# Input loaded in 2 KB rows and transposed before the norm, modulation matmuls of a whole column block in one burst, in a two-layer diffusion kernel

## The chip, the cores and the metric

The kernel runs on one core of a Trainium2 chip. The core has five engines that run their own lists of instructions in order and wait for each other by semaphores: TensorE (PE, matrix products into PSUM, with weight loads shown apart as PEld), VectorE (DVE), ScalarE (ACT), GpSimd (POOL) and SyncE (SP), which here only issues DMAs. Sixteen DMA engines move the data between HBM and the on-chip memory. The metric is the device time of one launch in microseconds. Three runs of the kernel before gave 2896.36, 2903.05 and 2905.09 us; the median is 2903.05.

## What is computed

Two layers of a diffusion backbone over 512 latent tokens `x` and 256 context tokens `ctx`, width 2048, all in float32. Each layer norms its input, modulates it by shift and scale that come from a vector `c` (latent) or `c_ctx` (context) through `w_ada`, projects it through `w_in` to queries, keys, values and a gate path z, runs three groups of attention heads, gates, projects back through `w_out` and adds the result to its input under a third modulation.

```python
shift, scale, gate = jnp.split(sc @ w_ada[l] + b_ada[l], 3, axis=-1)
...
h = rms(x, norm_w[l]) * (1.0 + scale[:, None]) + shift[:, None]
hc = rms(xc, norm_w[l]) * (1.0 + scale_c) + shift_c
...
qa, ka, va, qb, kb, vb, qc, kc, vc, z = project_stream(h, *weights, rope=(cos, sin))
```

`w_ada` is 2048 x 6144 for each layer, 50 MB in float32; shift and scale are its first two thirds, 33.5 MB. x is 4.2 MB and ctx 2.1 MB.

## The kernel before

Matrix products need the contracted dimension on the 128 partitions. So the normed, modulated input is kept transposed, as 16 k tiles `hT[.][k]`: 128 columns of the width on the partitions, the 768 tokens beside each other. Each float32 factor is split into a rounded half and the rest (`hi`, `lo`, or `wh`, `wl` for weights), and each product takes three matmuls: hi by hi, hi by lo, lo by hi (`mm`, line 333).

The start of layer 0 has these parts. `load_x` (line 854) loads x and ctx by k tile: 128 tokens by 128 columns, so rows of 512 bytes, two DMAs for each k tile; ACT squares it and DVE sums the squares by token. `ada_scale` (line 829) walks over shift and scale in blocks of 256 columns, alternating; `ada_blocks` (line 708) loads each block in eight tiles of 256 KB into the pool `s3` and multiplies them with the vectors in `scT` (line 743). Four tiles make one group of matmuls; up to 12 are loaded ahead. `ada_finish` brings the result onto the partitions (line 760), and `ada_use` adds the bias and makes the scale. `make_h` (line 870) waits for all squares, forms the norm's factor for each token, and `make_hk` multiplies a k tile by it, transposes it on PE (`tr`, line 336), and modulates it into `hT`.

The jobs of the projection then run in a list. In layer 0 the first is a pair: the first half (k tiles 0 to 7) of a key/value chunk and of a query chunk of 256 columns, in steps of two k tiles (`TJob.step`); the 72 matmuls of one such pair of steps have 256 columns each. Behind them stand three z jobs (`FJob`, 216 matmuls of 384 columns up to the end of modulation), then the second halves.

The order is made when the program is built. Strands (Python generators) put out instructions one by one, and a planner (`Weaver`) picks the next from a model of the engines' times; each engine then runs its list as it stands. All loads from HBM that matter here go through SP's one queue, in the order in which they were put out. A DMA into a buffer that is still read waits in SP's queue, and everything behind it waits too. The weights of the jobs come through `loader` and `splitter`: three buffers `ws` for loads, and two buffers `wl` for the rests, which come free when PE has used them. `RES` keeps some `s3` buffers back from the modulation's loads.

At the change of layers `post_out` (line 1872) makes the next input tile, its squares, and stores it to `xs1`.

## Time and profile before

| what | us |
|---|---|
| median of three runs | 2903.05 |
| the profiled execution | 2901.62 |
| its span | 2899.8 |
| PE busy in the span | 2775.4 |
| DVE busy in the span | 1995.0 |
| PE busy from 0 to 200 us | 154.0 |
| PE busy from 200 to 400 us | 197.3 |

The profile is of one execution. A line of a group names the line of the program, the engine, the operation, what it writes and reads and the shape; buffer numbers are left out, so `s` is any tile of the pool `s3`, `g` and `S` are PSUM tiles, `ws`, `wh`, `wl` the weights' tiles. Matmuls are pipelined, so their durations overlap; the distance between their starts is what one takes of PE's time. A timeline row gives start, duration, engine, line and operation, how many it merges, and in brackets the idle time before it with what ended it.

### The profile page before, as it was taken

The page shows a single profiled execution, that of the slowest core. Times are in us where ns is not written, and L with a number is a line of the kernel's source. Part 1 is how long each engine was busy: PE and PEld are TensorE (multiplying, and loading weights), DVE is VectorE, ACT ScalarE, POOL GpSimd, SP SyncE. Part 2 cuts the span into 40 slices and gives each one's busy share as a digit, 9 for nine tenths or more (in the row PEclk, how much of TensorE's full clock was granted, in tenths as well). Part 3 has the DMA queues.
Part 4 walks back from the last instruction along what each step waited for, and adds up shares of the span by engine and source line. Part 5 has one row for each costly group of instructions (what it writes and reads, how often), then busy time and mean ns, then how long its engine had stood idle before and what let it go on. Part 6 is the DMA issues. An engine that isn't in the chain of part 4 may idle for free.

```text
span 2899.8 us, 51534 instructions
## 1 busy us (share of the span) xinstructions
PE 2775.4 (96%) x19194; PEld 2604.4 (90%) x19194; DVE 1995.0 (69%) x5099; ACT 1220.0 (42%) x2652; POOL 155.4 (5%) x217
## 2 busy tenths in 40 slices
PE   5999999999999999989989999999999999999998
PEld 3779999999999999889989779999999898889977
DVE  5347676767897688989873385655657867598643
ACT  4223343433444355556322264333334545466421
POOL 3000000000010001000000000000001000000000
PEclk9999999999999999999999999999999999999999
DMA  9864434433233334324353453333333343412263
GB/s 256 254 202 112 116 90 122 112 103 113 87 86 111 107 113 134 108 80 149 125 161 108 131 152 107 109 98 103 109 110 93 105 117 110 117 45 95 88 175 117
DMA packets 393675, 349.92 MB, mean 121 GB/s; under 512 B 48004, under 2 KB 324274, under 8 KB 393424
## 3 DMA queue, kind: packets, MB, share of 16 engines
q1 hardware_dynamic: 391552, 345.31, 40.6%
q0 software_dynamic: 1872, 1.32, 0.5%
q8 instruction: 151, 2.47, 0.4%
q14 instruction: 100, 0.82, 0.1%
HBM read 305.01 MB, written 32.07 MB: 116 GB/s over the span
## 4 chain that ended last, share of the span: by engine, by line
PE 79%; DVE 10%; DMA 5%; issue 2%; SPq 2%; ACT 2%; DVEq 0%; ACTq 0%
PE g L333 62%; PE S L333 9%; PE g L336 5%; SPq L303 2%; DVE s L239 2%; DVE wl L239 2%; DVE s L272 1%; DMA s<-w_ada 1%; DVE ac L261 1%; DVE s L261 1%; ACT s L233 1%; DMA s<-scr 1%; DVE s L256 1%; PE g L801 1%; DVE tm L239 1%
## 5 line engine op out<-in xcount | busy, mean ns | idle before, releaser
L333 PE MATMUL g<-wh,s 128*128 128x256 f32 (+2 forms) x6248 | 1306.4, 298 | 18.1 <-DVE tm L239 6.4
L333 PEld LDWEIGHTS g<-wh,s 128*128 128x128 f32 x6248 | 1024.4, 192 | 46.5 <-ACT s L233 6.6
L333 PE MATMUL g<-wl,s 128*128 128x256 f32 (+2 forms) x3124 | 921.6, 295 | 5.4 <-DVE wl L239 5.0
L333 PE MATMUL g<-s,wh 128*128 128x384 f32 (+1 forms) x2688 | 762.5, 354 | 1.1 <-DVE s L239 0.6
L239 DVE TENSOR_TENSOR wl<-ws,wh 128x512 fp32r<-128x512 f32 (+1 forms) x606 | 417.6, 689 | 498.8 <-PE g L333 299.1
L333 PEld LDWEIGHTS g<-wl,s 128*128 128x128 f32 x3124 | 599.9, 192 | 20.0 <-DVE wl L239 10.8
L233 ACT ACTIVATE wh<-ws 128x512 fp32r<-128x512 f32 (+2 forms) x614 | 377.5, 616 | 431.3 <-PE g L333 344.4
L333 PEld LDWEIGHTS g<-s,wh 128*128 128x128 f32 x2688 | 492.2, 188 | 31.5 <-issue 2.1
L333 PE MATMUL g<-s,wl 128*128 128x384 f32 (+1 forms) x1280 | 448.3, 350 | 0.3 <-DVE wl L239 0.3
L233 ACT ACTIVATE s<-s,sm 128x512 f32<-128x512 f32 (+3 forms) x260 | 192.5, 740 | 460.6 <-DVE sm L272 375.2
L261 DVE SCALAR_TENSOR_TENSOR ac<-wa,scT,ac 128x512 f32<-128x512 f32 x420 | 309.2, 756 | 7.4 <-DMA wa<-w_ada 7.0
L333 PEld LDWEIGHTS g<-s,wl 128*128 128x128 f32 x1280 | 240.9, 188 | 12.4 <-DVE wl L239 0.6
L333 PE MATMUL S<-s,s 128*128 128x256 f32 (+3 forms) x1260 | 233.6, 314 | 16.4 <-DMA s<-s 8.7
L336 PE MATMUL g<-ident,s 128*128 128x128 f32 x1488 | 223.6, 277 | 12.9 <-DVE s L239 5.7
L333 PEld LDWEIGHTS S<-s,s 128*128 128x128 f32 x1260 | 188.5, 190 | 33.6 <-DVE sm L272 13.5
L333 PE MATMUL g<-pt,s 128*128 128x256 f32 (+1 forms) x1348 | 210.0, 285 | 8.7 <-DVE pt L239 6.2
L239 DVE TENSOR_TENSOR pt<-g,pt 128x512 fp32r<-128x512 f32 (+1 forms) x306 | 187.4, 623 | 44.2 <-ACT pt L233 42.2
L233 ACT ACTIVATE pt<-g 128x512 fp32r<-128x512 f32 (+1 forms) x306 | 160.4, 543 | 121.3 <-PE g L336 117.3
L233 ACT ACTIVATE tm<-g 128x512 f32<-128x512 f32 (+2 forms) x238 | 113.3, 494 | 212.9 <-PE g L333 134.2
L336 PEld LDWEIGHTS g<-ident,s 128*128 128x128 f32 x1488 | 174.3, 142 | 27.4 <-issue 6.1
L333 PEld LDWEIGHTS g<-pt,s 128*128 128x128 f32 x1348 | 185.4, 192 | 15.0 <-DVE pt L239 9.7
L282 POOL TENSOR_TENSOR s<-ot,s 64x256 f32<-64x256 f32 x100 | 88.3, 883 | 1473.3 <-DVE ot L239 1406.2
(157 smaller groups left out, 2453.7 us busy)
## 6 DMA issues: line engine op xcount, KB each, us to landing
ws<-w_in SPq DMA_DIRECT2D x288, 256.0 KB
wa<-w_ada SPq DMA_DIRECT2D x256, 256.0 KB
ws<-w_out SPq DMA_DIRECT2D x144, 256.0 KB
s<-w_ada SPq DMA_DIRECT2D x128, 256.0 KB
ws<-w_in SPq DMA_DIRECT2D x200, 128.0 KB
s<-scr SPq DMA_DIRECT2D x36, 384.0 KB
ws<-w_qb SPq DMA_DIRECT2D x54, 192.0 KB
s<-scr SPq DMA_DIRECT2D x40, 256.0 KB
```

What stands on the lines that cost most here:

```text
L233: self.nc.scalar.activation(out, in_, func, bias=bias, scale=scale, **kw)
L239: self.nc.vector.tensor_tensor(out, a, b, op=op)
L256: self.nc.vector.tensor_scalar(out, a, s1, s2, op0=op0, op1=op1)
L261: self.nc.vector.scalar_tensor_tensor(out, a, s, b, op0=op0, op1=op1)
L272: self.nc.vector.tensor_tensor_reduce(out, a, b, -1.0, init, OP.add, OP.min, acc)
L282: self.nc.gpsimd.tensor_tensor(out, a, b, op=OP.mult)
L303: self.nc.sync.dma_start(out, in_)
L333: self.nc.tensor.matmul(out, l, r, start=start, stop=stop, skip_group_check=True)
L336: self.nc.tensor.transpose(out, in_, self.ident)
L801: nc.tensor.matmul(pt[:, 2 * c + m:2 * c + m + 1], a[:, c * 128:(c + 1) * 128], one, start=c == 0 and m == sides[0], stop=c == n // 128 - ...
```

## The change

`load_x` now loads four columns of tiles, 512 columns wide: each DMA takes 128 tokens by 512 columns, rows of 2 KB, 256 KB in all; 24 DMAs instead of 32. `turn_x` transposes the raw tiles on PE, and DVE copies them from PSUM into the k tiles; `use_x` squares the untransposed tiles on ACT, which sums each row itself. `make_h`, for layer 0 alone, no longer touches the data: it forms the norm's factor by token, puts it on a diagonal, multiplies that with a matrix of ones on PE, and so gets a tile in which each partition holds the factor of all 768 tokens. `make_hk` multiplies the transposed tile by scale and by that tile in one DVE operation, adds the shift on ACT while it rounds, and forms the rest with one more DVE operation. Layer 1 keeps the old way under the names `make_h1` and `make_h1k`.

`ada_blocks` multiplies all tiles of a column block in one burst (eight loads of 256 columns, or four of 128), but in fours from column 1280 on; up to 16 tiles are loaded ahead once the norm's tile exists, eight until then. The first 256 columns are taken as two blocks of 128, whose rows are 512 bytes long. The first pair of jobs waits for single k tiles (`fine`) instead of two at once. The weight loader's loads are planned 2.5 us later, until the modulation is through. At the change of layers the store of a new tile is put out before the event that lets the next layer start on it.

```diff
-RES = dict(s3=8)
+RES = dict(s3=6)
...
+        self.margin = 2.5
...
+            w.cur.ft += self.margin
...
-            if self.evs is not None:
-                yield from K.wait(*(e for x in self.evs[self.k0 + m * p:self.k0 + m * p + m] for e in pick(x, ts[0] < 4, ts[-1] >= 4)))
-            yield from K.sync()
...
+                if kk == 0 or self.fine:
+                    if kk:
+                        K.w.pe(mmc(n) * 3 * len(ts))
+                        K.w.cur.ft = tp
+                        yield None
+                    if self.evs is not None:
+                        ev = self.evs[self.k0 + k:self.k0 + m * p + (kk + 1 if self.fine else m)]
+                        yield from K.wait(*(e for x in ev for e in pick(x, ts[0] < 4, ts[-1] >= 4)))
+                    yield from K.sync()
...
-    def ada_blocks(l, blocks, stag, ptag, depth, group):
+    def ada_blocks(l, blocks, stag, ptag, depth):
...
-        for i in range(0, len(items), group):
-            now = items[i:i + group]
-            c0, n, _ = now[0]
+        while items[nxt - len(pend):]:
+            i = nxt - len(pend)
+            c0, n, _ = items[i]
+
+            now = items[i:i + (4 if c0 % D >= 1280 else KT * n // 512)]
             if ps is None:
                 ps = yield from K.get(ptag)
-            while len(pend) < group:
-                while nxt < len(items) and len(pend) < depth and K.free(stag) > RES[stag]:
+            while len(pend) < len(now):
+                while nxt < len(items) and len(pend) < (depth if l in bcast else 8) and K.free(stag) > RES[stag]:
...
-    def ada_scale(l, n, stag, ptag, depth, group):
-        yield from ada_blocks(l, [(c + o, n) for c in range(0, D, n) for o in (0, D)], stag, ptag, depth, group)
+    def ada_scale(l, n, stag, ptag, depth):
+        cols = [(0, 128), (128, 128)] + [(c, n) for c in range(n, D, n)]
+        yield from ada_blocks(l, [(c + o, n) for c, n in cols for o in (0, D)], stag, ptag, depth)
...
     def load_x():
+
+        for c in range(4):
+            st = []
+            for i in range(6):
+                x = yield from K.get("s3")
+                w.cur.ft = w.vt
+                src = t["x"][0, i * 128:(i + 1) * 128] if i < 4 else t["ctx"][0, i * 128 - 512:i * 128 - 384]
+                tx = yield from K.load_ahead(x[:, :512], src[:, c * 512:(c + 1) * 512])
+                st.append((x, tx))
+            w.spawn(use_x(c, st), 0)
+
+    def use_x(c, st):
+        left = [4, 4]
+        for k in range(4 * c, 4 * c + 4):
+            xk[k] = yield from K.get("s3")
+        for k in range(4 * c, 4 * c + 4):
+            for seg in range(2):
+                w.spawn(turn_x(k, seg, st, left), 1)
+        sq = yield from K.get("s3")
+        for i, (x, tx) in enumerate(st):
+            w.cur.ft = max(w.vt, tx)
+            yield from K.act(sq[:, :512], x[:, :512], AF.Square, accum=ssx[:, c, i:i + 1])
+        K.put("s3", sq)
+        for e in ev_x[c]:
+            K.set(e)
+
+    def turn_x(k, seg, st, left):
+        a, b = SEG[seg]
+        w.cur.ft = max(tx for _, tx in st[a:b])
+        yield from K.token(("hl", "hc")[seg])
+        ps = yield from K.get("g")
+        yield from K.sync()
+        o = k % 4 * 128
+        for i in range(a, b):
+            K.tr(ps[:, (i - a) * 128:(i - a + 1) * 128], st[i][0][:, o:o + 128])
+        w.pe(0.109 * (b - a))
+        left[seg] -= 1
+        if left[seg] == 0:
+            K.put("s3", *(x for x, _ in st[a:b]))
+        yield from K.copy(xk[k][:, a * 128:b * 128], ps[:, :(b - a) * 128])
+        K.put("g", ps)
+        K.put(("hl", "hc")[seg], 0)
+        K.set(ev_t0[k][seg])
+
+    SEG = ((0, 4), (4, 6))
+
+    def make_h(l, evs, ev_h, seg):
+
+        a, b = SEG[seg]
+        c = slice(a * 128, b * 128)
+        ev_t = [ev_t0[k][seg] for k in range(KT)]
+        yield from K.wait(*(e[seg] for e in evs))
+        tot = yield from sm()
+        yield from K.red(tot[:, :b - a], ssx[:, :len(evs), a:b].rearrange("p k t -> p t k"))
+        yield from K.rsqrt(rx[:, a:b], tot[:, :b - a], 1.0 / D)
+        K.put("sm", tot)
+
+        dg = yield from K.get("tm")
+        yield from K.mul(dg[:, :(b - a) * 128].rearrange("p (t f) -> p t f", f=128), rx[:, a:b, None].to_broadcast([128, b - a, 128]),
+                         ident[:, None, :].to_broadcast([128, b - a, 128]))
+        ps = yield from K.get("g")
+        yield from K.sync()
+        for i in range(b - a):
+            nc.tensor.matmul(ps[:, i * 128:(i + 1) * 128], ones, dg[:, i * 128:(i + 1) * 128], start=i == 0, stop=i == b - a - 1,
+                             skip_group_check=True)
+        w.pe(0.22 * (b - a))
+        K.put("tm", dg)
+        if l not in bcast:
+            bcast[l] = [2 * KT, (yield from K.get("s3"))]
+        R = bcast[l][1]
+        yield from K.act(R[:, c], ps[:, :(b - a) * 128])
+        K.put("g", ps)
         for k in range(KT):
-            xk[k] = yield from K.get("s3")
-            w.spawn(load_xk(k), 0)
-
-    def load_xk(k):
-        v = xk[k].rearrange("p (t f) -> p t f", f=128)
-        yield from K.load(v[:, 0:4], t["x"][0, :, k * 128:(k + 1) * 128].rearrange("(t p) f -> p t f", p=128))
-        yield from K.load(v[:, 4:6], t["ctx"][0, :, k * 128:(k + 1) * 128].rearrange("(t p) f -> p t f", p=128), 131072)
-        sq = yield from K.get("s3")
-        yield from K.act(sq, xk[k], AF.Square)
-        yield from K.red(ssx[:, k, :], sq.rearrange("p (t f) -> p t f", f=128))
-        K.put("s3", sq)
-        K.set(ev_x[k][0])
-        K.set(ev_x[k][1])
-
-    def make_h(l, evs, ev_h, seg):
+            w.spawn(make_hk(l, k, ev_h, seg, ev_t[k], w.cur.ft), 2)
+            yield None
+
+    def make_hk(l, k, ev_h, seg, ev_t, tr):
+        a, b = SEG[seg]
+        c = slice(a * 128, b * 128)
+        n = (b - a) * 128
+        yield from K.wait(ev_t, ev_sh[l][k], ev_sc[l][k])
+        w.cur.ft = max(w.cur.ft, tr)
+        if seg == 0:
+            f = yield from K.get("s3", n=3)
+            hT[0][k], hT[1][k] = K.take("s3", F32R), K.take("s3", F32R)
+        else:
+            yield lambda: 0.0 if hT[0][k] is not None else None
+            f = yield from K.get("s3")
+        hi, lo = hT[0][k][:, c], hT[1][k][:, c]
+        sc, sh = gsc[l][:, k, seg:seg + 1], ada[l][:, k, seg:seg + 1]
+        yield from K.stt(f[:, :n], xk[k][:, c], sc, bcast[l][1][:, c], OP.mult, OP.mult)
+        yield from K.act(hi, f[:, :n], AF.Identity, bias=sh)
+        yield from K.stt(lo, f[:, :n], sh, r32(hi), OP.add, OP.subtract)
+        K.put("s3", f)
+        if seg == 1:
+            K.put("s3", xk[k])
+        bcast[l][0] -= 1
+        if bcast[l][0] == 0:
+            K.put("s3", bcast[l][1])
+        K.set(ev_h[k][seg])
+
+    def make_h1(l, evs, ev_h, seg):
...
+                        keep = w.cur.ft
+                        if 0 in sides:
+                            yield from K.store(xs1[:, k * 128:(k + 1) * 128].rearrange("(t p) f -> p t f", p=128),
+                                    xk[k][:, :512].rearrange("p (t f) -> p t f", f=128))
+                        w.cur.ft = keep
                         for x in sides:
                             K.set(ev_xn[k][x])
...
-                    if 0 in sides:
-                        for k in range(k0, k0 + nk):
-                            yield from K.store(xs1[:, k * 128:(k + 1) * 128].rearrange("(t p) f -> p t f", p=128),
-                                    xk[k][:, :512].rearrange("p (t f) -> p t f", f=128))
...
-                w.spawn(make_h(l, ev_in[l], ev_h, seg), 2)
+                w.spawn((make_h1 if l else make_h)(l, ev_in[l], ev_h, seg), 2)
...
+            kv[0].fine = q[0].fine = True
...
-        yield from ada_scale(0, 256, "s3", "g", 12, 4)
+        yield from ada_scale(0, 256, "s3", "g", 16)
+        K.margin = 0.0
```

What this does to the order. On SP, where the input ends and `w_ada` begins, there stood:

```order
L303 DMA s_212<-x 128x4x128
L303 DMA s_212<-ctx 128x2x128
L303 DMA s_214<-w_ada 128x2x256
L303 DMA s_321<-w_ada 128x2x256
L303 DMA s_326<-w_ada 128x2x256
```

and now at the same place (`s_199` to `s_373` are the four tiles of the first shift block, 128 columns wide):

```order
L308 DMA s_340<-ctx 128x512
L308 DMA s_346<-ctx 128x512
L308 DMA s_199<-w_ada 128x4x128
L308 DMA s_355<-w_ada 128x4x128
L308 DMA s_364<-w_ada 128x4x128
L308 DMA s_373<-w_ada 128x4x128
L308 DMA s_377<-w_ada 128x4x128
```

The input's rows are four times as long, and the first blocks' rows half as long; nothing else has come between them.

On PE, at the first projection matmuls, there stood (`s_209` is an input tile being transposed, `s_577` to `s_600` are tiles of `w_ada`, `s_661` and `s_662` the two halves of k tile 0):

```order
L336 MATMUL g<-ident,s_209 128x128 x2
L743 MATMUL g<-s_577,scT 32x256 x2
L743 MATMUL g<-s_586,scT 32x256 x2
L743 MATMUL g<-s_598,scT 32x256 x2
L743 MATMUL g<-s_600,scT 32x256 x2
L333 MATMUL g<-wh,s_661 128x256
L333 MATMUL g<-wl,s_661 128x256
L333 MATMUL g<-wh,s_662 128x256
```

and now (`s_377` to `s_408` are the four tiles of the first scale block, `s_632` and `s_633` the halves of k tile 0):

```order
L778 MATMUL g<-sel,tm 128x2
L938 MATMUL g<-tm,ones 128x128 x6
L761 MATMUL g<-s_377,scT 32x128 x4
L761 MATMUL g<-s_385,scT 32x128 x4
L761 MATMUL g<-s_399,scT 32x128 x4
L761 MATMUL g<-s_408,scT 32x128 x4
L778 MATMUL g<-sel,tm 128x2
L338 MATMUL g<-wh,s_632 128x256
L338 MATMUL g<-wl,s_632 128x256
```

All transposes now stand ahead of the modulation, and the first projection matmul stands behind two blocks of 128 columns. Before, it stood behind three blocks of 256 and behind most of the transposes.

Further on in PE's list, between projection matmuls, four tiles of `w_ada` made a group:

```order
L760 MATMUL g<-sel,tm 128x2 x2
L743 MATMUL g<-s_754,scT 32x256 x2
L743 MATMUL g<-s_772,scT 32x256 x2
L743 MATMUL g<-s_774,scT 32x256 x2
L743 MATMUL g<-s_776,scT 32x256 x2
L333 MATMUL g<-wh,s_871 128x256
```

and now eight do (`s_763` to `s_790` are the scale block of columns 256 to 511, `s_792` opens the next shift block):

```order
L338 MATMUL g<-wh,s_721 128x256
L761 MATMUL g<-s_763,scT 32x256 x2
L761 MATMUL g<-s_765,scT 32x256 x2
L761 MATMUL g<-s_768,scT 32x256 x2
L761 MATMUL g<-s_770,scT 32x256 x2
L761 MATMUL g<-s_772,scT 32x256 x2
L761 MATMUL g<-s_776,scT 32x256 x2
L761 MATMUL g<-s_778,scT 32x256 x2
L761 MATMUL g<-s_790,scT 32x256 x2
L778 MATMUL g<-sel,tm 128x2 x2
L761 MATMUL g<-s_792,scT 32x256 x2
```

A whole block now stands in one piece, and the next shift block directly behind the scale block that it follows. Up to the end of the modulation PE's list holds the same projection matmuls before and after: 288 of 256 columns and 216 of 384. From there on its order is the same in both until the change of layers, where some matmuls and some of SP's loads and stores change places, and again from there to the end.

More of the change, by code (lines that the diff above doesn't have):

```diff
@@ L240, in tt, with copy @@
         self.w.bump("dve", 0.07 + 0.00104 * self.n(out))
+    def copy(self, out, a):
+        yield from self.gate("dve")
+        self.nc.vector.tensor_copy(out, a)
+        self.w.bump("dve", 0.07 + 0.00104 * self.n(out))
     def mul(self, out, a, b):
@@ L440, in __init__ @@
         self.done = [Event() for _ in self.banks]
-        self.inS = False
+        self.inS = self.fine = False
     def specs(self):
@@ L626, in body @@
     sel = K.st([128, 2], name="sel")
-    one = K.st([128, 1], name="one")
-    nc.vector.memset(one, 1.0)
+    ones = K.st([128, 128], name="ones")
+    nc.vector.memset(ones, 1.0)
+    one = ones[:, 0:1]
     maskA = K.st([128, 640], BF16, name="maskA")
@@ L731, in ada_blocks @@
                         K.set(ev_go)
-                if len(pend) >= group:
+                if len(pend) >= len(now):
                     break
@@ L744, in ada_blocks @@
                                      skip_group_check=True)
-            w.pe(0.3 + 0.215 * group)
+            w.pe(0.4 + 0.26 * len(now))
             K.put(stag, *(s for s, _ in tiles))
@@ L850, in body @@
     xk = [None] * KT
[L851 removed]
+    ev_x = [(Event(), Event()) for _ in range(4)]
+    ev_t0 = [(Event(), Event()) for _ in range(KT)]
     hT = [[None] * KT, [None] * KT]
     def load_x():
[L855 to L868 removed]
@@ L879, in make_h, with make_h1k @@
             yield from K.token(("hl", "hc")[seg])
-            w.spawn(make_hk(l, k, ev_h, seg, a, b), 2)
+            w.spawn(make_h1k(l, k, ev_h, seg, a, b), 2)
             yield None
-    def make_hk(l, k, ev_h, seg, a, b):
+    def make_h1k(l, k, ev_h, seg, a, b):
         v = xk[k].rearrange("p (t f) -> p t f", f=128)
```

4 lines of the change are left out of this document (2 added, 2 removed).

## The prediction, made before the changed kernel ran

> **What bounds the kernel now.** I read the page first.
>
> ```profile
> span 2899.8 us, 51534 instructions
> PE 2775.4 (96%) x19194; PEld 2604.4 (90%) x19194; DVE 1995.0 (69%) x5099; ACT 1220.0 (42%) x2652; POOL 155.4 (5%) x217
> PE   5999999999999999989989999999999999999998
> DMA  9864434433233334324353453333333343412263
> ```
>
> PE is full in every slice but the first, and that is the only stretch in which the DMA engines are full. So a change to the start is worth what it takes out of the start: PE works its list in order, and what comes earlier there moves everything behind it. The stages of the start, by windows (columns: stage, length, busy time of each engine, granted clock, DMA share, GB/s):
>
> ```profile
> 0.00:34.50 34.50, 1.27 (x5) 0.88 (x5) 15.10 (x19) 15.32 (x23) 18.39 (x39) 1.00 1.00 224
> 34.50:58.10 23.60, 22.25 (x194) 14.75 (x194) 22.75 (x71) 16.05 (x38) 9.68 (x4) 1.00 1.06 334
> 58.10:184.70 126.60, 117.53 (x985) 92.06 (x983) 39.06 (x92) 34.16 (x65) 0.51 (x1) 0.99 0.81 252
> ```
>
> PE does nothing for 34.5 us, then 23.6 us of preparation (transposes and modulation) before the first projection matmul, and in the third stage it is busy while DMA rests a fifth of the time. The borders are rows of the timeline:
>
> ```profile
> 33.66 0.84 ACT L233 ACTIVATE s<-s 128x768 f32<-128x768 f32 x1 [0.41 <-DMA s<-ctx]
> ...
> 52.27 1.07 PE L743 MATMUL g<-s,scT 128*32 128x256 f32 x16
> ...
> 55.14 0.55 DVE L256 TENSOR_SCALAR s<-s,gsc,ada 128x512 f32<-128x512 f32 x1
> ...
> 58.16 0.39 PE L333 MATMUL g<-wh,s 128*128 128x256 f32 x1
> ...
> 184.70 0.42 PE L333 MATMUL g<-s,wh 128*128 128x384 f32 x1
> ```
>
> The last input tile lands at about 33; the second modulation block gets PE at 52.27, between transposes, though its loads are long in; the first normed tile is made from 55.14 on; projections run from 58.16; 184.70 is the first matmul after the last block of modulation. The waits say who held whom:
>
> ```profile
> PE g L743 <- ACT s L233: 24.8, 1, 24.8
> PE g L743 <- DMA s<-w_ada: 4.4, 6, 1.2
> SPq L303 <- DVE wl L239: 43.5, 14, 6.2
> ```
>
> PE's one long wait, 24.8 us, ends with the input. Afterwards it hardly waits for w_ada (4.4 us): a backlog stood ready at 58. And SP's queue stood 43.5 us of the first 200 behind a weight tile whose buffer was not free, with w_ada loads queued behind it.
>
> **The yardstick.** In the order of the changed kernel PE has the same 288 matmuls of 256 columns and 216 of 384 columns before the end of the last modulation block, then the same 72 before the next job; after that PE's order is that of before up to the change of layers. So the sum is the time at which PE reaches the point that was 184.70.
>
> **1. The input.** 512-byte rows become 2 KB rows. Packets of both lengths nearest to it, from the DMA view of 4 to 16 us (input) and of 44 to 66 us (w_ada):
>
> ```profile
> q1 hardware_dynamic: 5781, 2.84, 91.2%
> q0 software_dynamic: 500, 0.16, 23.3%
> ...
> DMA packets 7640, 7.34 MB, mean 334 GB/s; under 512 B 470, under 2 KB 7573, under 8 KB 7635
> ...
> q1 hardware_dynamic: 7550, 7.01, 100.1%
> ```
>
> 91.2% of 16 engines for 12 us is 175 us for 5781 packets of 491 B: 30.3 ns each, 259 GB/s. The second is 352 us for 7550 packets of 928 B: 46.7 ns. The line through both gives 91 ns for 2048 B (an estimate beyond its ends). 6.29 MB are 12288 packets before, 23.3 us on 16 engines, and 3072 after, 17.5 us. It saves 5.8 us; bounds 0 (all of it hidden by the small POOL transfers, unchanged) and 8 (if the share of those, 23% of the engines in the first window, shrinks too). I take 5.5: the input is in at 27.5, and w_ada follows at once.
>
> By the Trainium skill's "DMA: Bandwidth & Descriptors", section Specifications, 512 B is enough for line rate, so longer rows would save nothing; by that rule the sum loses these 5.5 us. The two rows above speak against it: 259 GB/s in 491 B packets.
>
> **2. From 27.5 on, supply.** Now the first block pair is 128 columns wide and no transpose waits for a norm, so k tile 0 needs 2.1 MB of w_ada, not 4.2. It lands at 27.5 + 2.1/0.259 = 35.6; with its finish, scale and split (3 us from 55.14 to 58.16) and 2 us of block matmuls, the first projection stands near 41 instead of 58.16. But there is no backlog: two k tiles need 16 loads (4.19 MB at 334 GB/s, 12.6 us) and two weight tiles (0.52 MB, 1.9 us), 14.5 us. What PE does for them:
>
> ```profile
> 94.10 0.40 PE L333 MATMUL g<-wh,s 128*128 128x256 f32 x2
> 94.34 0.28 PE L333 MATMUL g<-wl,s 128*128 128x256 f32 x1
> 94.46 0.40 PE L333 MATMUL g<-wh,s 128*128 128x256 f32 x2
> ...
> 111.06 1.07 PE L743 MATMUL g<-s,scT 128*32 128x256 f32 x16
> 112.06 0.39 PE L333 MATMUL g<-wh,s 128*128 128x256 f32 x1
> ```
>
> Three matmuls per 0.36 us, so 72 take 8.6; four loads of modulation take 1.0, so two bursts of eight 4.0; with their small finishing matmuls 13.3 us. Supply sets the pace up to k tile 7. The order puts the matmuls of k tiles 6 and 7 behind the shift block of columns 1024 to 1279. Up to it 72 w_ada loads and 11 weight tiles must land: 5.6 MB in 512-byte rows (16 loads of w_ada, half the weights) at 259 GB/s, 21.6 us, and 16.1 MB at 334, 48.3 us: 27.5 + 69.9 = 97.4. Behind that 8.6 for the pair, 2.1 for the scale block within it and 2.0 for a slow clock (next part): **110.1**.
>
> **3. The clock.** Where PE had waited shortly, the matmuls behind it took twice as long:
>
> ```profile
> 105.18 0.64 PE L743 MATMUL g<-s,scT 128*32 128x256 f32 x8
> 106.78 1.84 PE L743 MATMUL g<-s,scT 128*32 128x256 f32 x8 [0.97 <-DMA s<-w_ada]
> 108.56 0.58 PE L333 MATMUL g<-wh,s 128*128 128x256 f32 x1
> ...
> 100.00:120.00 20.00, 17.85 (x152) 13.69 (x155) 5.57 (x13) 6.69 (x13) 0.00 (x0) 0.91 1.00 318
> ```
>
> The same eight records took 1.84 instead of 0.64, and the granted clock of the stage is 0.91: about 2 us lost. The change makes such waits, one for each pair (14.5 against 13.3). While loads set the pace the loss is hidden in the wait; the last one is not. So once 2.0; bounds 0 and five times.
>
> The Trainium skill, "TensorE: Matmul & The Clock Gate", section HAM oscillation, says that a PE which idles some 3.4 us per tile starts each tile at half clock: it speaks against this change. In this trace a wait of 0.97 us, with a shorter one just ahead, was enough.
>
> **4. From 110.1 on, PE again.** The z jobs and the remaining blocks were this before:
>
> ```profile
> 122.01 1.07 PE L743 MATMUL g<-s,scT 128*32 128x256 f32 x16
> 123.01 0.44 PE L333 MATMUL g<-s,wh 128*128 128x384 f32 x1
> ...
> 174.96 1.07 PE L743 MATMUL g<-s,scT 128*32 128x256 f32 x16
> ```
>
> From 122.01 to 174.96, 53.0 us, PE did all 216 matmuls of 384 columns and 10 groups of modulation; before the new end stand 12 groups, 55.2 us, and the finish 0.5: 110.1 + 55.7 = **165.8**. The loads hide behind it: 56 of w_ada at 334 GB/s, 44 us, and nine weight tiles, 9.1, end at 97.4 + 53.1 = 150.5, a cushion of 15 us. Before, PE used up its work at 176 and went on at 184.70. Gain: 184.7 - 165.8 = 18.9.
>
> **5. What is late next.** Behind the last block the chain to the last h tile is longer on DVE: two operations with two tensors instead of one and a cheap one.
>
> ```profile
> 185.54 0.55 DVE L256 TENSOR_SCALAR s<-s,gsc,ada 128x512 f32<-128x512 f32 x1
> ...
> 186.38 0.69 DVE L239 TENSOR_TENSOR s<-s,s 128x512 fp32r<-128x512 f32 x1 [0.30 <-ACT s L233]
> ...
> L261 DVE SCALAR_TENSOR_TENSOR ac<-wa,scT,ac 128x512 f32<-128x512 f32 x420 | 309.2, 756 | 7.4 <-DMA wa<-w_ada 7.0
> ```
>
> 1.51 instead of 1.24 us for 512 columns, over two tiles and both segments about 1 us; between 0 and 2. The rest lies beside the first w_ada loads: the last of 32 copies out of PSUM and of 24 squares (some 5 us behind the last input tile, at about 0.7 each), the norm's chain, and six matmuls with ones. The chain's price is its own before:
>
> ```profile
> 35.52 0.38 DVE L266 TENSOR_REDUCE sm<-ssx 128x4 f32<-128x64 f32 x2
> ...
> 38.81 0.15 DVE L261 SCALAR_TENSOR_TENSOR rx<-sm,rx 128x2 f32<-128x2 f32 x1
> ```
>
> 27.5 + 5 + 3.4 and 1 to 2 for the ones: near 37.5. The first scale block, in at 35.6, is ready at 38.5, so nothing shows; without that cover up to 3 us would, once, and PE's next burst waits for loads until 46 anyway. The weight loads' margin only keeps them from standing in SP's queue; its cost is the same cushion.
>
> **6. The change of layers.** The store of each new tile is issued earlier, past SP's weight loads, and some matmuls swap places. PE's largest wait there:
>
> ```profile
> PE g L333 <- DVE tm L239: 6.4, 4, 2.7
> ```
>
> Nothing prices the swaps; at best they save half of the 6.4, at worst they add as much: 3 either way, taken as 0.
>
> **Sum.** 18.9 - 1.0 = 17.9 off the profiled execution's 2901.6 (span 2899.8 and 1.8 around it): 2883.7, so 2884. That execution lies 1.4 under the median of its three runs, 2903.05.
>
> **Rivals.** (a) The input isn't faster, or each wait of PE costs its 2 us of slow clock: gain 17.9 - 5.5 = 12.4, or 17.9 - 8 = 9.9, so 2889 to 2892. For it: the POOL transfers share the engines, and 106.78 shows the loss. Against it: a slow PE eats its own wait. (b) Slower: bursts free eight buffers at once and late, so SP stands behind a buffer, and supply sinks. At the 252 GB/s of the third stage the 38.8 MB from 27.5 on take 154 us, and the loads end at 181.5 and PE at 183 to 184: no gain. That is the point: below some 250 GB/s it is slower; at the 224 GB/s of the first stage the loads end at 201 and PE at 203, 18 later than before: 2920. For it: the 43.5 us of SP's waits. Against: in the new order sixteen loads, 12.6 us, stand ahead of a burst, and the weight tiles stand behind more of them. (c) More: the waits are short, the clock stays full, the input saves 8 us: gain 23 to 28, 2874 to 2879. (d) The change doesn't do what it says, because the DMA engines set the pace with or without 2 KB rows: that is (a)'s first half.
>
> **How the numbers follow.** The forecast, 2880 to 2888, 0.55; (a) 2888 to 2894, 0.22; a mix of (a) and the start of (b), within 0.3%, 0.11; (b) slower, 0.05; (c) 0.07. A difference of 0.3% (8.7 us) is about what a measurement of this kernel tells from none. Faster by more than it: 0.55 + 0.22 + 0.07, less a little of (a) at its edge: 0.83; within 0.12; slower 0.05. The range leaves out (b) and the far ends: 2874 to 2897.
>
> **What would show it.** Right: input in at 27 to 28 us; first projection at 39 to 43; then PE waiting for w_ada several us per pair until about 97; z jobs without waits; the old 184.70 at 164 to 168; the rest of the span unchanged. Wrong: DMA share far under 0.9 between 28 and 97 us (b), matmuls of 0.24 us pitch through whole pairs (a), or the gain present at 200 us and gone at 1700.

## The result and the profile after

The changed kernel takes **2877.89 us** (median of 4 runs, 2875.56 to 2879.84), beside it the kernel before 2899.82 (median of 4). The ratio is 0.9915, with a 95% interval from 0.9902 to 0.9928: it is faster by 22 us. Measured a second time, beside the experiments, it took 2882.57 (6 runs, 2876.95 to 2886.96) against 2904.08, ratio 0.9926 [0.9912, 0.9939], 21.5 us. The forecast was 2884, with a range from 2874 to 2897. One execution of run 7 below took 4523.53 us at a granted clock of 0.555 and is left out of that run's times.

The page of the changed kernel, its busiest engine and the slices (tenths of 40 equal parts of the span):

```profile
span 2873.8 us, 51646 instructions
PE 2774.4 (97%) x19270; PEld 2610.4 (91%) x19270; DVE 1985.4 (69%) x5088; ACT 1209.1 (42%) x2656; POOL 147.9 (5%) x217
PE   7999999999999999899999999999999999999998
PEclk8999999999999999999999999999999999999999
DMA  9853434333233334325353443333333333413253
```

PE's first slice rose from 5 to 7, and DMA is as full as it was there. New is an 8 in the granted clock's first slice. The same three stages as before, by windows (stage, length, busy time of PE, its weight loads, DVE, ACT and POOL, granted clock, DMA share, GB/s):

```profile
0.00:34.50 34.50, 20.45 (x134) 15.48 (x135) 19.15 (x58) 19.21 (x56) 17.59 (x37) 0.89 0.95 250
34.50:58.10 23.60, 17.86 (x168) 13.50 (x169) 8.71 (x28) 5.10 (x12) 3.08 (x7) 0.65 1.13 324
58.10:184.70 126.60, 118.48 (x1025) 99.56 (x1024) 52.70 (x107) 37.37 (x73) 0.66 (x2) 1.00 0.83 261
```

PE now transposes while the input arrives: 20.45 us of work in a stretch that held 1.27. In the second stage it works less than before (17.86 against 22.25) and at a clock of 0.65. The 1.00 of before in that stage must be read with care. The clock's records begin at 42.3 us in that trace (at 13.3 in this one), and the column counts all ahead of them as full. Yet before's transposes ran at half their later pace there:

```profile
38.95 3.25 PE L336 MATMUL g<-ident,s 128*128 128x128 f32 x14 [1.22 <-DVE s L239]
...
44.70 1.95 PE L336 MATMUL g<-ident,s 128*128 128x128 f32 x16
```

That is 0.23 us for each of the first and 0.12 for each of the second. The rows of the changed kernel's timeline that answer to those of before:

```profile
29.33 0.63 ACT L233 ACTIVATE s<-s 128x512 f32<-128x512 f32 x1 [0.39 <-DMA s<-ctx]
...
35.78 2.90 PE L938 MATMUL g<-tm,ones 128*128 128x128 f32 x12 [0.88 <-DVE tm L239]
38.61 1.94 PE L761 MATMUL g<-s,scT 128*32 128x128 f32 x32
...
43.36 0.38 PE L338 MATMUL g<-wh,s 128*128 128x256 f32 x1 [1.99 <-ACT s L233]
...
98.14 1.93 PE L761 MATMUL g<-s,scT 128*32 128x256 f32 x32
...
116.06 0.42 PE L338 MATMUL g<-s,wh 128*128 128x384 f32 x1
...
169.30 0.61 PE L778 MATMUL g<-sel,tm 128*128 128x2 f32 x4 [0.50 <-ACT tm L233]
169.77 0.43 PE L338 MATMUL g<-s,wh 128*128 128x384 f32 x1
...
185.74 0.28 PE L338 MATMUL g<-wh,s 128*128 128x256 f32 x1
```

The last input tile is in at 29.3 (33.7 before), the first projection matmul stands at 43.36 (58.16), the first z job at 116.06, and the first matmul behind the last modulation block at 169.77 (184.70): a gain of 14.9. 185.74 is the first matmul of the job behind z, so the lead is 15.0 there; before, it was

```profile
200.70 0.28 PE L333 MATMUL g<-wh,s 128*128 128x256 f32 x1
```

The experiments are compared at that row, since PE's order is the same in all of them from there to the change of layers. PE's waits in the first 200 us (line, releaser, total, times, longest), and the one of SP's queue that was quoted of before:

```profile
PE g L341 <- DMA s<-x: 6.8, 4, 4.4
PE g L338 <- ACT s L233: 5.6, 5, 2.0
PE g L341 <- DMA s<-ctx: 4.6, 3, 2.4
PE g L778 <- ACT tm L233: 3.7, 7, 0.8
...
PE g L761 <- DMA s<-w_ada: 1.3, 2, 0.8
```

```profile
SPq L308 <- DVE wl L239: 36.7, 14, 8.1
```

The transposes (L341) wait for the input itself. Behind that PE hardly waits for `w_ada`. It waits for ACT: for the h tile behind a scale block, 2.0 us at a time, and for the copy ahead of a block's finish.

The whole of the profiled pair differs by 26.0 us in span. Matched matmul by matmul the lead is 15.0 us at 200 us, 14.6 at 437 of before, 20.8 at 1589, 18.4 at 1690, 23.6 at 1990 and 25.8 at the last matmuls. So 15 us come from the start and 11 from behind it, and 5.8 of these are there by 1589 us, ahead of the change of layers, in a stretch in which no engine's order differs from before. The experiments had to tell where both come from.

### The profile page after: what moved, and what is told of

Its sections match the earlier page's. It is cut to its first block, busy times and chain, and to the rows that moved or that the text cites. A ratio compares the mean times of both kernels' runs of the same rounds, so it can differ in the third digit from the quotient of the medians.

```text
span 2873.8 us, 51646 instructions
## 1 busy us (share of the span) xinstructions
PE 2774.4 (97%) x19270; PEld 2610.4 (91%) x19270; DVE 1985.4 (69%) x5088; ACT 1209.1 (42%) x2656; POOL 147.9 (5%) x217
## 4 chain that ended last, share of the span: by engine, by line
PE 82%; DVE 10%; DMA 3%; issue 2%; ACT 2%; SPq 1%; DVEq 0%; ACTq 0%
PE g L338 65%; PE S L338 10%; PE g L341 5%; DVE s L239 2%; DVE wl L239 1%; DVE s L266 1%; DVE s L277 1%; PE g L761 1%; DVE ac L266 1%; ACT s L233 1%; PE g L819 1%; DVE tm L239 1%; DVE s L261 1%; DVE pt L239 1%; SPq L308 1%
## 5 line engine op out<-in xcount | busy, mean ns | idle before, releaser
L341 PE MATMUL g<-ident,s 128*128 128x128 f32 x1488 | 225.4, 279 | 22.8 <-DMA s<-x 6.8
L341 PEld LDWEIGHTS g<-ident,s 128*128 128x128 f32 x1488 | 176.6, 143 | 35.6 <-issue 8.4
L233 ACT ACTIVATE tm<-g 128x384 f32<-128x384 f32 (+4 forms) x240 | 113.4, 491 | 205.5 <-PE g L338 131.3
L338 PEld LDWEIGHTS g<-pt,s 128*128 128x128 f32 x1348 | 184.5, 191 | 14.5 <-DVE pt L239 8.9
```

Source lines behind the costliest of these rows:

```text
L233: self.nc.scalar.activation(out, in_, func, bias=bias, scale=scale, **kw)
L338: self.nc.tensor.matmul(out, l, r, start=start, stop=stop, skip_group_check=True)
L341: self.nc.tensor.transpose(out, in_, self.ident)
```

## The experiments

Twelve runs. "Lead" is the row at 185.74 in the changed kernel's first profile minus the same row of the run: positive is sooner than the changed kernel. Two more profiles have the changed kernel's start unaltered, and their row stands at 186.62 (run 2) and 186.94 (run 5); the start of before gave 200.70 and, in run 1, 201.89. So a lead is known to about 1.2 us, and a cost measured from 185.74 is at its upper end.

**1 and 2. The stores at the change of layers, alone and undone.** In the kernel before:

```diff
                         K.put("s3", sq)
+                        keep = w.cur.ft
+                        if 0 in sides:
+                            yield from K.store(xs1[...], xk[k][...])
+                        w.cur.ft = keep
                         for x in sides:
                             K.set(ev_xn[k][x])
-                    if 0 in sides:
-                        for k in range(k0, k0 + nk):
-                            yield from K.store(xs1[...], xk[k][...])
```

> The kernel before with one part of the change alone: at the change of layers the store of each new tile is issued right behind its squares and not behind all of the block. All else is the kernel before. Aligned matmul by matmul, the two profiled executions are 14.9 us apart at 200 us, 14.6 at 440, 20.8 at 1590, 18.4 at 1690, 23.6 at 1990 and 25.8 at the end, though between 200 and 1640 us no engine's order differs. Theory A (the store is worth something): about 4 to 5 us faster than the kernel before, all of it between 1690 and 2040 us, 2895. Theory B (everything behind 200 us is the difference between two executions): within 1.5 us of the kernel before, and the drift between 200 and 1640 us appears against the first profile of before in this run too.

Measured 2901.66 us beside 2901.89, ratio 0.9997 [0.9987, 1.0007]: nothing. And with the same edit undone in the changed kernel:

> The changed kernel with that one part undone: the stores stand behind all of the block again. Theory A: 4 to 5 us slower than the changed kernel, 2882 to 2883, the loss between 1690 and 2040 us. Theory B: 2877 to 2879, no difference. Under both the first 200 us are those of the changed kernel: first matmul behind the last modulation block at 169 to 171 us.

Measured 2883.76, ratio to before 0.9940 [0.9925, 0.9956]; the row stands at 186.62. That looked like 6 us against 2877.89, but the changed kernel measured again (run 5) takes 2882.57. The ratios, 0.9940 here and 0.9926 there, have intervals that overlap. By both runs the stores are worth nothing that can be told from zero, and theory A falls. The first pair's jump at the change of layers is not theirs.

**3. The input in short rows.** The tiles get gaps, so that a contiguous piece is 512 bytes:

```diff
-tx = yield from K.load_ahead(x[:, :512], src[:, c * 512:(c + 1) * 512])
+tx = yield from K.load_ahead(x.rearrange("p (a g) -> p a g", g=192)[:, :, :128],
+                             src[:, c * 512:(c + 1) * 512].rearrange("p (a f) -> p a f", f=128))
```

> The changed kernel, whose input loads now write four strips of 128 columns with gaps between them, so that one contiguous piece is 512 bytes and not 2 KB; no engine's order differs from the changed kernel but for the shape in these 24 loads. Theory A (step 1 of the prediction: short rows cost 30.3 ns for 491 bytes): the input lands about 4 to 5 us later, at 33 to 34 us and not at 29.3, the first projection matmul at 47 to 48 and not at 43.4, and the whole is 3 to 5 us slower than the changed kernel, 2881 to 2883. Rival (the small constants of GpSimd, which fill half of the DMA time between 16.5 and 22 us, set the end of the input whatever the rows): input in within 1 us of 29.3, time within 1.5 us of the changed kernel.

The last input tile came at 34.49, the first projection at 47.81, the row at 189.73. The DMA views of 12 to 16.5 us (packets, MB, share of 16 engines), first with short rows, then in the changed kernel:

```profile
q1 hardware_dynamic: 2058, 1.02, 87.8%
```

```profile
q1 hardware_dynamic: 884, 1.60, 95.7%
```

87.8% of 16 engines for 4.5 us over 2058 packets is 30.7 ns for 496 bytes; the second is 77.9 ns for 1.8 KB. Theory A: rows of 2 KB save 5.2 us at the input's end and **4.0** at the row, and the whole takes 2887.61, ratio 0.9950 [0.9936, 0.9965]. By the ratios that is 7 us more than the changed kernel's second measurement, whose interval it just touches.

**4 and 6. GpSimd's constants out of the input's way.** From 12 to 16.5 us all DMA of the changed kernel moved 364 GB/s; right behind it, from 16.5 to 22 us, the changed kernel moved this:

```profile
DMA packets 434, 0.73 MB, mean 133 GB/s; under 512 B 78, under 2 KB 78, under 8 KB 434
## 3 DMA queue, kind: packets, MB, share of 16 engines
q0 software_dynamic: 88, 0.09, 50.7%
q1 hardware_dynamic: 346, 0.64, 49.3%
```

88 packets of the small constants take as much engine time as 346 of the input. So they were held back, on GpSimd, behind a scale vector of a later k tile (k tile 7 in run 4; 9 for tables and masks, 15 for norm weights and sinks in run 6):

```diff
 def small():
+    if l == 0:
+        yield from K.wait(ev_sc[0][15])
+        nc.gpsimd.tensor_copy(hold, gsc[0][:, 15, :])
...
 def rpb_prep():
-    yield from K.wait(ev_c)
+    yield from K.wait(ev_sc[0][9])
+    nc.gpsimd.tensor_copy(hold, gsc[0][:, 9, :])
```

> The changed kernel with GpSimd's small constant loads (norm weights, sinks, bias tables and masks; not those that the modulation needs) held back until k tile 7 has its scale, some 100 us. In the changed kernel's profile the input moves at 364 GB/s between 12 and 16.5 us and at 133 GB/s between 16.5 and 22, where half of the engines' time goes to 88 packets of these constants. Theory A: without them the input lands 3 to 5 us sooner, at 24.5 to 26.5, the first projection at 38.5 to 41, and the whole is 3 to 5 us faster than the changed kernel, 2873 to 2875. Rival (PE is the limit from 50 us on, and the slow clock eats what comes earlier): input sooner, but the first matmul behind the last modulation block within 1.5 us of 169.8 and the time within 1.5 us of the changed kernel. Third: the slow stretch is not the constants' doing, and the input still lands at 28 to 30.

> The changed kernel with the small constants held back further than in the run before: the bias tables and masks until k tile 9 has its scale, some 125 us, the norm weights and sinks until k tile 15 has it, some 165. There the constants came at 80 to 120 us, beside w_ada loads that PE waited for, and a lead of 5.8 us at the first projection matmul (37.5 instead of 43.4) was down to 0.2 at 127 us. Theory A (the lead was lost to the constants themselves, moved into a stretch that still needs its loads): first projection at 37 to 38 again, the lead at 127 us 3 to 6 us, the whole 3 to 5 us faster than the changed kernel run beside it. Theory B (the lead is lost because loads, or the buffers that they wait for, set the pace between 60 and 115 us): lead at 127 us under 1.5 us and no gain in the whole.

In run 4 the same 5.5 us moved 2.02 MB at 367 GB/s, the first projection stood at 37.54 (5.8 sooner), and by 127 us the lead was 0.2, at the row 1.8: the constants, now at 80 to 120, lay beside loads that PE waited for (0.8 us at 113.5). 2879.64, ratio 0.9920 [0.9904, 0.9937]. In run 6 the first projection is 6.6 sooner and the lead stays at **3.2**; 2875.97, ratio 0.9910 [0.9896, 0.9923], 6.6 less than the changed kernel measured in the same session, though their intervals overlap. Half of the lead went where the chain from modulation to h tile stood bare:

```profile
62.90 0.39 PE L338 MATMUL g<-wh,s 128*128 128x256 f32 x1 [1.99 <-ACT s L233]
...
64.79 3.29 PE L761 MATMUL g<-s,scT 128*32 128x256 f32 x32
```

A wait of 1.99 us, and behind it a burst at half clock: 3.29 instead of 1.93. Together 3.4 us. In the changed kernel the planner had put the next burst in that place, so that PE had work while the h tile was made:

```profile
67.42 0.61 PE L778 MATMUL g<-sel,tm 128*128 128x2 f32 x4 [0.59 <-ACT tm L233]
67.96 1.93 PE L761 MATMUL g<-s,scT 128*32 128x256 f32 x32
```

**5. The changed kernel again.**

> The changed kernel itself once more, beside the other runs. Its first profile is 14.9 us ahead of before at 200 us and 25.8 at the end, and the three kernels with edits in the first 110 us alone drifted by 1 to 7 us against it between 200 and 1640 us, where no engine's order differs. Theory A (between 200 us and the end executions differ by some us, through stretches of half clock of 3.4 us each that fall on other waits each time): this profile is within 0.5 us of the first at 200 us, 2 to 7 us behind it at 1640, and the median is 2878 to 2882. Theory B (the later gain belongs to the change): the same times as in the first profile within 1 us all along, median 2877 to 2879, and the kernel with the stores put back, 2883.8, is 5 us slower for its stores.

The median is 2882.57; the profile's row stands at 186.94, a lead of -1.2, and its span is 2885.2. Against the first profile it loses 3.3 us between 1405 and 1505 alone. The windows there, first of the first profile, then of this one:

```profile
1480.00:1520.00 40.00, 33.12 (x260) 32.19 (x259) 30.04 (x54) 8.71 (x13) 0.00 (x0) 0.96 0.52 155
```

```profile
1480.00:1520.00 40.00, 34.50 (x239) 33.31 (x238) 28.36 (x50) 8.73 (x14) 0.00 (x0) 0.83 0.50 154
```

The granted clock is 0.96 in the one and 0.83 in the other. Theory A in kind, and more than it said in size (8.6 us behind at 1640): with this profile as the pair's second half, 13.8 us of gain come from the start and 0.8 from all the rest, with the first it was 15.0 and 11.0. From the row to the end of the span the nine profiles with this order behind it (the first one, runs 3 to 6 and 8 to 11) take 2688.1 to 2698.3 us; the lowest is the first profile, the highest this one.

This spread goes with the clock. Behind the row the trace records half clock for 22.6 us in the first profile, for 49.1 in this one and for 27.8 to 42.4 in the other seven, and the time behind the row rises with it, by about 0.36 us for each us at half clock (a straight line through the nine). The kernel before doesn't lie on that line: it has 29.9 us at half clock, for which the line gives 2690.7, and takes 2699.1.

**7 and 11. Wide first blocks.**

```diff
-cols = [(0, 128), (128, 128)] + [(c, n) for c in range(n, D, n)]
+cols = [(c, n) for c in range(0, D, n)]
```

> The changed kernel with modulation blocks of 256 columns from the start: the four narrow blocks of 128 are two of 256 again. Theory A (step 2 of the prediction: the first k tile needs 4.2 MB of w_ada instead of 2.1, 2.1 MB at 334 GB/s are 6.3 us): the first projection matmul at 48 to 51 instead of 43.4, and most of it stays, the first matmul behind the last modulation block at 173 to 176 instead of 169.8, the whole 3 to 6 us slower than the changed kernel. Rival (PE idles a third of the time between 31 and 51 us anyway, and what it does there later isn't more): first projection later, but the yardstick within 1.5 us.

> The kernel with blocks of 256 columns from the start again, for its profile and a second set of times. Theory A: first projection matmul at 48 to 51 instead of 43.4, the first matmul behind the last modulation block at 173 to 176 instead of 169.8 to 171. Rival: the first projection later, the second within 1.5 us of 171.

Run 7's profile is of the execution at 4523.53 us, so it serves for its other five times alone. Of run 11's timeline:

```profile
49.59 0.58 PE L338 MATMUL g<-wh,s 128*128 128x256 f32 x1 [1.99 <-ACT s L233]
...
169.71 0.43 PE L338 MATMUL g<-s,wh 128*128 128x384 f32 x1
```

The first projection is 6.2 us later, as 2.1 MB at 334 GB/s would have it, and nothing of it is left at 169.71 (169.77 in the changed kernel). It is gone long before: the 37th projection matmul stands at 59.5 in run 11 and at 60.5 in the changed kernel, whose PE waits once more, until 51.10, for the second 128 columns. In this profile the narrow blocks are worth **0.0**: the rival. The times don't quite say so, 2886.26 (median of five) and 2886.13, ratios 0.9940 [0.9924, 0.9956] and 0.9932 [0.9918, 0.9946], against 0.9915 and 0.9926; run 11's profiled run was one of its fastest. A loss of a few us in other executions stays possible.

**8. Groups of four.**

```diff
-now = items[i:i + (4 if c0 % D >= 1280 else KT * n // 512)]
+now = items[i:i + 4]
```

> The changed kernel with modulation in groups of four loads in all columns, no bursts of eight. Theory A (a burst of eight takes PE 1.93 us, two groups of four 2 x 1.07, and each return to projections costs some 0.1 more; seven bursts): 1 to 3 us slower at the first matmul behind the last modulation block, the same in the whole. Theory B (rival b of the prediction: bursts free their buffers late, and SP stands behind them, 5.4 us between 28 and 120): with groups of four SP's waits for PE's modulation shrink by half or more and the block is reached 2 us sooner.

The row stands at 189.66, **3.9** later; 2884.47, ratio 0.9938 [0.9925, 0.9951]. 1.2 of it is there at the first projection already and not the groups' doing. The rest is more than theory A's arithmetic: one group waits for its load in the middle,

```profile
54.01 0.62 PE L761 MATMUL g<-s,scT 128*32 128x256 f32 x4 [2.75 <-DMA s<-w_ada]
```

which a burst, placed later, would perhaps not have done; that was not tested. Theory B is refuted: SP's waits for PE's modulation did shrink, from 5.4 to 1.7 us between 28 and 120, but the block was not reached sooner.

**10. No margin for the weight loads.**

```diff
-self.margin = 2.5
+self.margin = 0.0
```

> The changed kernel with the weight loads' margin at zero from the start (2.5 in the changed kernel until the modulation of layer 0 is done), so that they are issued sooner among the w_ada loads. Theory A (the margin keeps SP from standing behind weight buffers): SP waits more than 45 us of the first 200 for weight buffers (36.7 in the changed kernel), PE waits for w_ada some 2 to 4 us, and the first matmul behind the last modulation block comes 1 to 4 us later than 169.8 to 171. Theory B (PE is the limit there, and the prediction gave the margin no term): within 1 us of it, and the whole within 2 us of the changed kernel.

The row stands at 190.55, **4.8** later; 2885.24, ratio 0.9939 [0.9926, 0.9953]. 1.0 of it is there at the first projection. SP stands no longer behind weight buffers than in the changed kernel (34.2 us against 36.7), so theory A's mechanism isn't it, and theory B's 1 us is passed. What the windows show, from 30 to 80 and 80 to 130 us, first of this run, then of the changed kernel:

```profile
30.00:80.00 50.00, 39.42 (x363) 29.86 (x362) 20.43 (x70) 11.93 (x26) 4.03 (x8) 0.73 1.05 317
80.00:130.00 50.00, 46.83 (x454) 39.23 (x454) 19.17 (x41) 15.96 (x31) 0.00 (x0) 1.00 0.78 240
```

```profile
30.00:80.00 50.00, 40.37 (x403) 31.97 (x405) 20.28 (x68) 10.31 (x23) 4.03 (x8) 0.83 1.11 327
80.00:130.00 50.00, 46.78 (x460) 38.18 (x456) 19.10 (x40) 16.02 (x31) 0.00 (x0) 1.00 0.92 288
```

In the first window the clock is lower, 0.73 instead of 0.83: 5 us of full clock in 50. In the second fewer loads come (240 GB/s instead of 288), but PE is as busy there as in the changed kernel. So the loss is in the first: the 109th projection matmul, ahead of which both have done the same modulation, stands 5.3 us later, at 82.0 instead of 76.7. The place is that of run 6. Without the margin the planner leaves the chain to the h tile bare again:

```profile
71.79 0.58 PE L338 MATMUL g<-wh,s 128*128 128x256 f32 x1 [1.99 <-ACT s L233]
...
73.91 3.64 PE L761 MATMUL g<-s,scT 128*32 128x256 f32 x32
```

The wait of 1.99 us and a burst that takes 3.64 instead of 1.93 are 3.7 us, and 1.0 was there before: together the 4.8, nearly. In this profile the margin works through the order that the planner makes.

**9. The clock held up.** On top of run 6, 46 transposes of the identity into a spare PSUM buffer, where PE waits:

```diff
+def fill(n):
+    if not K.free("g"):
+        return
+    dm = K.take("g")
+    for _ in range(n):
+        K.tr(dm[:, :128], ident)
+    K.put("g", dm)
...
+if l == 0 and c0 in (D, D + 128, D + 256):
+    fill(14)
...
+if seg == 0:
+    fill(18)
```

> The kernel with the constants held back twice as far (the run at 2875.97), with 46 transposes of the identity into a spare PSUM buffer put where PE waits there: 18 ahead of the norm's matmuls with ones, 14 behind the finish of each of the first two scale blocks. No engine's order differs but for these. There PE waits 2.8, 2.0 and 2.0 us at these places, and stretches of half clock lie at 30 to 33, 37 to 40, 44 to 51 and 64 to 67 us; a burst took 2.77 to 3.29 us in them, 1.93 outside. Theory A (short waits bring the half clock, and it costs PE work on the path): the stretches ahead of 60 us are gone or shorter, the second projection k tile comes 2 to 4 us sooner, and 1.5 to 4 us of it are left at the first matmul behind the last modulation block. Theory B (another limit takes over, the loads or the chain from modulation to h tile): clock full, but under 1 us left there. Theory C (transposes don't hold the clock): half clock as before, and the additions cost up to 3 us.

The windows, first of run 6, then of this run:

```profile
30.00:60.00 30.00, 25.23 (x254) 20.42 (x254) 8.34 (x20) 6.76 (x15) 0.00 (x0) 0.77 1.05 316
60.00:70.00 10.00, 7.25 (x59) 4.91 (x60) 4.74 (x10) 3.44 (x7) 0.00 (x0) 0.83 0.99 324
```

```profile
30.00:60.00 30.00, 24.41 (x286) 19.29 (x286) 9.81 (x24) 7.07 (x16) 0.00 (x0) 1.00 1.06 321
60.00:70.00 10.00, 9.22 (x65) 6.52 (x66) 3.63 (x8) 3.03 (x6) 0.00 (x0) 0.66 1.10 345
```

The clock is full up to 60 us; the third place, near 60, had no buffer free for its transposes, and there the half clock still comes. PE is 2.3 us ahead of run 6 at 54 us and 1.2 at the row (181.28). So the half clock does lie on the path, though half of what it costs is hidden again: between theories A and B in size, A in mechanism, and C is refuted. 2872.73 us, ratio **0.9892** [0.9877, 0.9907]: the fastest of all, and the only faster one whose interval lies clear of the changed kernel's second one. It overlaps those of run 6 and of the changed kernel's first.

**12. Everything but the layout undone.** Run 3's edit, with:

```diff
-RES = dict(s3=6)
+RES = dict(s3=8)
-self.margin = 2.5
+self.margin = 0.0
-now = items[i:i + (4 if c0 % D >= 1280 else KT * n // 512)]
+now = items[i:i + 4]
-(depth if l in bcast else 8)
+depth
-cols = [(0, 128), (128, 128)] + [(c, n) for c in range(n, D, n)]
+cols = [(c, n) for c in range(0, D, n)]
-kv[0].fine = q[0].fine = True
-yield from ada_scale(0, 256, "s3", "g", 16)
+yield from ada_scale(0, 256, "s3", "g", 12)
```

> The changed kernel with everything else of the change undone together: input in 512-byte pieces, blocks of 256 columns from the start, groups of four, no margin, the reserve of 8 buffers and the depth of 12 as before, and the waits of the first jobs for pairs of k tiles. What stays is the raw transposing with the norm in the transposed layout, and the early stores. The changed kernel is 14.9 us ahead of before at the first matmul behind the last modulation block; one at a time, short rows cost 4.0 of it, groups of four 3.9, no margin 4.8, wide blocks 0.0. Theory A (the parts add up): 12.7 of the 14.9 are gone, the block's end at 181 to 184 us (184.7 before), the whole within 3 us of before run beside it. Theory B (the parts stand for one another, and the norm's wait taken out of the start is the core): 6 to 10 us ahead of before at that point and in the whole. In two of those profiles the input landed 2 us later by chance, so that up to 4 of the 12.7 isn't the parts' own: 4 to 6 ahead would be in between.

The row is only 0.5 ahead of before:

```profile
200.16 0.28 PE L338 MATMUL g<-wh,s 128*128 128x256 f32 x1
```

The time is 2900.58 us beside 2903.47, ratio 0.9989 [0.9979, 0.9999]. Theory A. (The later input that the expectation allows for is smaller than it says: 30.39 and 30.28 us in runs 8 and 10, against 29.33.) The raw transposes and the norm in the transposed layout bring next to nothing alone. The start's gain lies in the other parts. The reserve, the depth and the single waits were undone only here, all at once, and whether the parts would bring as much without the new layout was not run.

## Why the prediction was right, step by step

The time was right, and the sum nearly: 17.9 us were to come from the start, 15.0 and 13.8 came in the two profiles. But the measured gain, 21.5 to 22 us, holds some 7 us from behind the start that no step forecast; that the whole came out so near is partly luck. The steps that made up the sum did worse than the sum. Of the prediction's own signs of being right only the z jobs without waits came; the input's end, the first projection (43.36, not 39 to 43), PE's waits for `w_ada` and the old 184.70 (169.77, not 164 to 168) missed, most of them narrowly, and the rest of the span, which was to stay, differs by 0.8 to 11.0 us.

**1, the input: right.** 5.5 us forecast, 5.2 measured by undoing it (run 3), and 30.3 ns for a short packet against 30.7. The line through its two packets gives 89 ns for 2048 bytes, not 91, so the step's own 5.8 us should have been 6.3. The input's end was 29.3, not 27.5: while GpSimd's constants load, which the step had named only for its bounds, all DMA together moves 133 GB/s for 5.5 us. The rule of the Trainium skill's "DMA: Bandwidth & Descriptors", section Specifications, that 512 bytes are enough for line rate, doesn't hold here: 16 engines at run 3's 30.7 ns for 496 bytes move 259 GB/s, at 77.9 ns for 1.8 KB 372, and the row is 4.0 us later with rows of 512 bytes.

**2, supply: the place right, the reason wrong.** The first projection stands at 43.4 (41 forecast; the input explains 1.8 of 2.4). The burst that was to land at 97.4 runs at 98.14. But PE was to wait several us per pair for `w_ada` and waits 1.3 in all. From 58 to 116 us DMA and PE are both nearly full:

```profile
58.00:116.00 58.00, 52.78 (x542) 43.55 (x541) 19.54 (x42) 17.32 (x34) 0.51 (x1) 1.00 0.99 311
```

A pair was to take PE 13.3 us, under the 14.5 of its loads. With its waits for ACT and DVE it takes as much or more: pairs begin at 70.03, 85.75 and 100.54, 15.7 and 14.8 us apart. The narrow blocks bring the first projection forward, as the step says, but nothing behind it (run 11). Nor do their short rows cost what the step's sum has for them, 16 loads at 259 GB/s instead of 334, 3.6 us: run 11 has no such gain either. Bursts and margin, which it passed over as free, bring 2.7 to 3.9 and 3.6 to 4.8 by the three rows of the unaltered start, if one execution each can be trusted for so much.

**3, the clock: size near, cause and place wrong.** The 2.0 us were to be lost at a wait for a load. They are lost before 60 us, at waits for the chain from modulation to h tile (2.0 us each): the granted clock is 0.65 from 34.5 to 58.1. Run 9 gives 1.2 us on the path, on top of run 6. The Trainium skill's "TensorE: Matmul & The Clock Gate", section HAM oscillation, had the right direction, though less than its 3.4 us of idling is enough here: the half clock comes at waits of 2.0 to 2.8 us, and filling them ends it.

**4, the z jobs: right.** From 116.06 to 169.77 without a wait until the last block's finish, 53.7 where 55.7 was forecast. They begin 6 us late. Behind the burst at 98.14 the step forgot the burst's own 1.9, the four short waits of 2.4 for ACT and DVE (100.5 to 109.5 us), and the first group of the next block with its finish, 1.5, which the order puts ahead of z and which the z jobs then save; the 2.0 for the clock wasn't spent there. With the burst's own delay of 0.7 that is 4.5 of the 6.0; the rest isn't placed.

**5, the longer chain behind the last block: nothing** (1.0 forecast, 0 to 2). The lead is 14.9 ahead of it and 15.0 behind.

**6, the change of layers: right**, 0 within 3 (runs 1 and 2).

**What the sum did not hold:** the first pair's 11 us behind 200 us. Run 5 shows that executions alone can differ by as much: with one program, 2688.1 us behind the row in one and 2698.3 in the other, with more half clock in the second. Yet the medians are 21.5 to 22 us apart, 7 more than the start shows, and the three profiles that reach the row at 200 us or later (before, runs 1 and 12) take 2698.3 to 2699.1 behind it, at the upper end. The clock is not why: before has less half clock there than seven of the nine profiles, and the highest granted clock of all, 0.995. With runs 1 and 2 the start's part lies between 13.8 and 16.2, so it is 5 to 8 us that stay open; no run tells where they come from.

Of the rivals, (b) has nothing for it: the rate from 58 to 116 us is 311 GB/s, and where it falls to 240 behind 80 us, without the margin, the time had been lost before. (a) and (c) each have their half: the clock is lost, and the input could save more, but only with the constants out of its way.

## What to carry to other kernels

An earlier start is not a gain until it is followed to the place where the limits meet: of 6.2 us at the first projection nothing was left 17 us later, of 6.6 about half by 91 us. An edit that only shifts a planner's times can change the order, and so uncover a wait that was hidden: a wait of 2 us and the slow burst behind it cost 3.4 us in run 6 and 3.7 in run 10. Look at who else uses the DMA engines while a critical input lands; 88 packets of constants cost as much as 346 of the input, and they could wait. And before two profiles are compared far from the edit, take one of the two kernels twice.

## What the runs showed of the hardware

Software-queue packets can be dear: 88 of them took 50.7% of 16 engines for 5.5 us, 0.5 us each, while the 346 input packets beside them took 0.13 us each. Others are not: 194 of them between 12 and 16.5 us took 10.4%, 0.04 us each. Moving the dear ones lifted what all DMA moved in that window from 133 to 367 GB/s.

The granted clock falls to half in short stretches after waits of 1 to 3 us, also far from any edit, and not in the same places each time: 0.83 against 0.96 in the same 40 us of the same program. Over nine profiles each us at half clock went with about 0.36 us more time. A PE kept busy with transposes that nobody reads held 1.00 over 30 us where it had 0.77.
